# The order of SyncE's transfer queue in the convolution module of a two-layer diffusion trunk

## The chip, the cores and the metric

The kernel runs on one core of a Trainium2 chip. The metric is device time in microseconds (us) of one execution, as the median of several; three runs of the kernel before gave 1317.1, 1321.2 and 1324.15 us. The profile is of one further execution. Engines are named as in the profile: PE (TensorE, matrix products), DVE (VectorE), ACT (ScalarE), POOL (GpSimd) and SP (SyncE, whose queue issues the transfers).

## The reference

Two layers over 256 tokens of width 1024, in float32. Layer 0 is a mixer (mLSTM heads and differential attention) and a dense SwiGLU. Layer 1 is a Conformer convolution module and a top-2-of-8 expert SwiGLU. The change is in the convolution module, of which this is the core:

```
u = modulate(x, mix_pre_g, sh_m, sc_m)
a, g = jnp.split(u @ pw1_w + pw1_b, 2, axis=-1)
h = a * jax.nn.sigmoid(g)
h = depthwise_conv(h, dw_w) + dw_b          # 31 taps along the tokens, per channel
h = jax.nn.silu(layernorm(h, ln_g, ln_b))
y = h @ pw2_w + pw2_b
```

After it come the norm, the router, and the experts, whose weights (eight experts of three matrices) are most of what the kernel reads.

## The kernel before

**Weights.** All weights lie in HBM as units of 128 x 2048 floats (1 MB). `raw` (L330) asks for a unit with one transfer issued by SP, into a ring of six buffers ("raw" and "raw2" in the rows). `half` (L363) splits half a unit into a high part (ACT, L372, tile `whi`) and a low part (DVE, L373, tile `wlo`), and PE multiplies with both. `Ahead` (L380) keeps a list of such halves for the first projection pw1, eight units of two halves: `step` makes the next half, asking for its unit with the first, and `get` returns a half that is due. Five halves are made before the stage, so each step makes the half that PE uses five products later. A buffer is asked for anew once DVE has taken both halves out of it (or, for a unit of taps, PE).

**The stage (L1422 to L1481).** The channels are eight blocks k of 128. The loop over `jj` = 0 to 3 computes two blocks of `a` and two of `g` a turn, in four products of half a unit (24 matmuls each). After the first product of the next turn, `glu(jj - 1)` forms a * sigmoid(g) for blocks k = 2 jj - 2 and 2 jj - 1: ACT makes the sigmoid (L1416, L1417), DVE multiplies into `hp[k]` (L1418).

**The depthwise convolution.** Blocks 0 and 1 are convolved on DVE: `conv_v` (L1359) is one tensor_scalar (L1361) and 30 scalar_tensor_tensor (L1364), which are queued as "background" and put between other work by `fill(n)`, n at a time. Blocks 2 to 7 are convolved on PE: `conv_shift(k)` (L1343) writes `hp[k]` to a scratch tile `hd` in HBM (L1345) and reads it back four times, shifted by 0 to 3 tokens, into `x4` (L1348, "B<-hd" in the profile); `conv(k)` (L1350) then multiplies it with a unit of taps, 64 matmuls in the trace. `x4` has three buffers, k modulo 3. The units of taps `w4s[jj]` are asked for at the start of turns 1, 2 and 3.

**What follows a block.** `convolved` (L1381) takes the results. After the second of them, a product with `on` (in the trace "mm<-B,on") gives their mean over channels, the pilot, which ACT copies (L1399) and DVE subtracts from both (L1401); every later block has it subtracted as it leaves PSUM (L1390). The first two are blocks 0 (from DVE) and 2 (from PE). `sums` adds up each block and its square on PE ("aux<-B,one", "aux<-m,one").

**What sets the order.** A scheduler places the instructions of every engine by priorities and dependencies, except where `in_order` stands around them: there the named engines keep the order of the source. Around this stage it names PE, DVE and ACT. SP is not named, so the transfers stand where the scheduler put them. Each engine works its queue off strictly from the front, and SP's queue too: a transfer that waits for a semaphore holds up all that stand behind it. The units of the second projection pw2 are asked for outside this stretch of the source, and the scheduler may move them, and their halves, into it.

PE's order in the stage: pw1 for turns 0 to 2; the first unit of turn 3; conv(2), the pilot's product and its sums; the last unit of pw1; conv(3), conv(4), conv(5); then conv(6) and conv(7) with the sums between.

Of the kernel before, what the change touches and what calls it, by code (L numbers as in the profile page):

```python
# [11 lines left out]
F32 = mybir.dt.float32  # L12
# [7 lines left out]
P = 128  # L20
D = 1024
KT = D // P
T = 256
# [8 lines left out]
HW = T + 32  # L32
# [6 lines left out]
NV = 2  # L39
# [197 lines left out]
def build(ctx: ExitStack, tc: tile.TileContext, d, unit, dbg=None):  # L237
    nc = tc.nc
# [5 lines left out]
    def nm(s):  # L244
        ctr[0] += 1
        return f"{s}_{ctr[0]}"
# [83 lines left out]
    def raw(key, src=None, two=False):  # L330

        src = d["w"][unit[key]] if src is None else src
        tag = room.pop(0) if room else "raw"
        if tag in ("gp", "w", "xn", "pT"):
            if tag == "w":
                t = [ring("whi", F32, HW_), ring("wlo", F32, HW_)]
            else:
                t = [tl([P, HW_], "gp"), tl([P, HW_], "m4")] if tag == "gp" else [tl([P, HW_], tag, bufs=2) for _ in range(2)]
            for q in range(2):
                nc.sync.dma_start(t[q], src[:, HW_ * q : HW_ * q + HW_])  # L340
            return t
        t = ring("raw") if tag == "raw" else tl([P, UW], tag)
        if two:
            for q in range(2):
                nc.sync.dma_start(t[:, HW_ * q : HW_ * q + HW_], src[:, HW_ * q : HW_ * q + HW_])
        else:
            nc.sync.dma_start(t, src)
        return t[:, :HW_], t[:, HW_:]
# [148 lines left out]
    def fill(n=1000):  # L497

        while background and n > 0:
            if next(background[0], 0) == 0:  # L500
                background.pop(0)
            else:
                n -= 1
# [134 lines left out]
    ET = mybir.EngineType  # L638

    def in_order(*engines):  # L640
        return tc.manual_schedule(engines=set(engines or (ET.PE, ET.DVE, ET.Activation)))
# [119 lines left out]
    def wstat(half, out, n0, n1):  # L761
        h, l = by_k(half, KT)
        for k in range(KT):
            mm(out, h[:, k], uh[k][:, n0:n1], k == 0, False)
            mm(out, h[:, k], ul[k][:, n0:n1], False, False)
            mm(out, l[:, k], uh[k][:, n0:n1], False, k == KT - 1)
# [573 lines left out]
    cvo = tl([P, KT, T], "B8")  # L1340


    def conv_shift(k):  # L1343
        hd = hdram.tile([P, HW], F32, tag="hd", name=nm("hd"), bufs=4)
        nc.sync.dma_start(hd, hp[k])  # L1345
        x4 = x4s[k % 3]
        for j in range(4):
            nc.sync.dma_start(x4[32 * j : 32 * j + 32], hd[:, j : j + HW - 4].rearrange("(c p) t -> p c t", c=4))  # L1348

    def conv(k):  # L1350
        w4 = w4s[k // 2][k % 2].rearrange("p (b c) -> p b c", c=32)
# [53 lines left out]
    w4s = {}  # L1405
# [13 lines left out]
            if k < NV:  # L1419
                background.append(conv_v(k))  # L1420

    order = in_order()  # L1422
    order.__enter__()
    pp = None
    for jj in range(4):
        if jj >= NV // 2:
            w4s[jj] = raw(("taps", jj))
        prev, pp = pp, []
        for n in (jj, 4 + jj):
            p_ = pm("mm")  # L1430
            for j in range(2):
                ahead.step()
                wstat(ahead.get(("pw1", n), j), p_[:, T * j : T * j + T], 0, T)
                if prev:
                    glu(jj - 1, prev)
                    if jj > 1:
                        conv_shift(2 * jj - 2)
                    if jj != 3 and jj > 1:
                        conv_shift(2 * jj - 1)
                    prev = None  # L1440
                    fill(2)
                else:
                    fill(4)
            pp.append(p_)
            fence.close()
            if jj == 3 and n == jj:
                conv(2)
                drain(2)
                conv_shift(5)
    conv(3)  # L1450
    drain(2)
    glu(3, pp)
# [865 lines left out]
```

## Time and profile before

| | |
|---|---|
| median of three runs | 1321.2 us (1317.1 to 1324.15) |
| profiled execution | 1319.89 us, its span 1317.9 us |
| mean granted clock of PE in it | 0.978 of full speed |
| busy in the span | PE 1254.1 us (95%), DVE 633.0 (48%), ACT 431.2 (33%) |
| bytes | 406.41 MB, mean 308 GB/s |
| convolution stage | about 472 to 560 us of the span |

How to read it: PE is the engine that is nearly always busy, so a change counts for what it adds to or takes from PE's waits, or from the time in which PE runs at the lower clock. Times in a row are microseconds from the start of the span. "[4.00 <-DMA B<-hd]" behind a row is the time that the engine stood idle before it, and what ended it. "SPq" rows are issues of transfers: their length is what the issue takes and not the transfer, whose time to landing is listed apart. [...]

### The profile page before, as it was taken

What the parts mean: (1) busy time and instruction counts of PE and PEld (TensorE: products, weight loads), DVE (VectorE), ACT (ScalarE), POOL (GpSimd) and SP (SyncE); (2) the same over time, 40 slices, a digit from 0 to 9 for tenths busy, and PEclk for the clock granted to TensorE, in tenths of its full rate; (3) what the DMA queues carried; (4) which work ended last, traced back from release to release, by engine and by line L of the source; (5) the groups of instructions that cost most, each with busy time, mean ns of one, the idle gap of its engine ahead of it and who ended that gap; (6) DMA issues with size and microseconds to landing.
All of it is one profiled execution on the core that took longest, in us unless ns stands there. A gap on an engine that the chain in (4) does not pass through costs nothing. (4 is left out here: it accounts for less than half of the span.)

```text
span 1317.9 us, 22697 instructions
## 1 busy us (share of the span) xinstructions
PE 1254.1 (95%) x9256; PEld 807.2 (61%) x9256; DVE 633.0 (48%) x1049; ACT 431.2 (33%) x784; POOL 32.4 (2%) x83
## 2 busy tenths in 40 slices
PE   6999999999999998998999789999999999999996
PEld 5878777789998987674345333444434444678533
DVE  4689758698886668663102012011111121689422
ACT  4553346564444553262020000210001102567311
POOL 1000001100000010011000000000000000000000
PEclk9999999999999999997999899999999999999998
DMA  9727820478987627687769999999999996999994
GB/s 353 283 95 297 309 98 9 160 313 347 361 324 308 255 76 206 213 275 292 264 260 417 420 420 418 419 419 368 360 418 420 419 372 263 426 347 368 350 419 191
DMA packets 71089, 406.41 MB, mean 308 GB/s; under 512 B 7874, under 2 KB 12226, under 8 KB 31812
## 3 DMA queue, kind: packets, MB, share of 16 engines
q1 hardware_dynamic: 70980, 404.91, 78.5%
q8 instruction: 74, 1.21, 0.4%
q14 instruction: 35, 0.29, 0.1%
HBM read 402.94 MB, written 1.93 MB: 307 GB/s over the span
## 5 line engine op out<-in xcount | busy, mean ns | idle before, releaser
L373 DVE TENSOR_TENSOR wlo<-raw,whi 128x1024 fp32r<-128x1024 f32 x154 | 186.0, 1222 | 47.6 <-ACT whi L372 46.5
L282 PE MATMUL mm<-raw,gL 128*32 128x256 f32 (+3 forms) x1392 | 194.0, 438 | 4.5 <-DMA raw<-w 4.5
L372 ACT CAST whi<-raw 128x1024 fp32r<-128x1024 f32 x154 | 159.4, 1048 | 102.6 <-PE mm L282 64.3
L282 PE MATMUL mm<-B,whi 128*128 128x256 f32 x960 | 171.8, 282 | 0.2 <-DVE B L632 0.2
L282 PEld LDWEIGHTS mm<-B,whi 128*128 128x128 f32 x960 | 148.4, 189 | 2.3 <-PE mm L282 0.6
L282 PE MATMUL mm<-B,wlo 128*128 128x256 f32 x480 | 134.9, 281 | 0.0
L282 PE MATMUL mm<-B,gL 128*32 128x256 f32 (+3 forms) x808 | 124.4, 449 | 3.3 <-DMA B<-w 3.3
L282 PEld LDWEIGHTS mm<-raw,gL 128*32 128x32 f32 (+1 forms) x1392 | 77.9, 122 | 80.8 <-issue 57.5
L1887 DVE TENSOR_TENSOR cv<-cv,mm 64x512 f32<-64x512 f32 (+1 forms) x36 | 23.3, 647 | 191.4 <-ACT cv L1886 191.1
L1886 ACT ACTIVATE cv<-mm 64x512 f32<-64x512 f32 (+1 forms) x36 | 19.9, 553 | 280.9 <-PE mm L282 280.8
L282 PE MATMUL aux<-whi,pT 128*128 128x512 f32 (+2 forms) x400 | 100.9, 425 | 0.6 <-DMA whi<-w 0.6
L282 PEld LDWEIGHTS mm<-B,wlo 128*128 128x128 f32 x480 | 90.6, 189 | 0.0
L282 PEld LDWEIGHTS mm<-B,gL 128*32 128x32 f32 (+1 forms) x808 | 46.7, 123 | 55.3 <-issue 40.8
L282 PE MATMUL aux<-raw,pT 128*32 128x256 f32 (+1 forms) x592 | 77.6, 470 | 1.6 <-DMA raw<-w 0.9
L282 PE MATMUL aux<-wlo,pT 128*32 128x256 f32 (+2 forms) x284 | 69.1, 429 | 1.9 <-DVE wlo L373 1.1
L1903 DVE COPY pT<-aux 128x384 f32<-128x384 f32 (+4 forms) x42 | 19.0, 453 | 107.8 <-PE aux L1896 99.1
L282 PEld LDWEIGHTS aux<-whi,pT 128*128 128x128 f32 (+2 forms) x400 | 49.5, 158 | 25.5 <-issue 13.2
L282 PE MATMUL mm<-U,whi 128*128 128x256 f32 (+1 forms) x240 | 64.5, 331 | 0.0
L282 PE MATMUL aux<-B,pT 128*32 128x256 f32 (+2 forms) x424 | 59.7, 467 | 0.0
L282 PE MATMUL mm<-whi,B 128*128 128x512 f32 (+1 forms) x192 | 58.4, 380 | 0.0
L282 PE MATMUL mm<-whi,gL 128*32 128x256 f32 (+3 forms) x336 | 55.9, 452 | 2.3 <-DMA whi<-w 2.3
L282 PE MATMUL mm<-wlo,gL 128*32 128x256 f32 (+3 forms) x336 | 53.9, 445 | 0.2 <-DMA wlo<-w 0.2
(467 smaller groups left out, 1866.9 us busy)
## 6 DMA issues: line engine op xcount, KB each, us to landing
raw<-w SPq DMA_DIRECT2D x237, 1024.0 KB, 7.5
B<-w SPq DMA_DIRECT2D x69, 1024.0 KB, 11.2
whi<-w SPq DMA_DIRECT2D x52, 512.0 KB, 11.3
wlo<-w SPq DMA_DIRECT2D x52, 512.0 KB, 10.9
gp<-w SPq DMA_DIRECT2D x18, 512.0 KB, 10.1
m<-w SPq DMA_DIRECT2D x18, 512.0 KB, 10.0
B<-hd SPq DMA_DIRECT2D x24, 142.0 KB, 5.3
x<-x SPq DMA_DIRECT2D x2, 512.0 KB, 4.4
```

The source lines that it names most:

```text
L282: PE.matmul(out, lhsT, rhs, start=start, stop=stop)
L372: A.copy(hi, rq)
L373: V.tensor_tensor(lo, rq, f(hi), ALU.subtract)
L1886: A.activation(s, p_[:64, :w], AF.Silu)
L1887: V.tensor_tensor(s, s, p_[64:, :w], ALU.mult)
L1903: V.tensor_copy(h[:, :o], pt[:, :o])
```

## The change

`in_order` now names SP too, so that the transfers of the stage stand in the order of the source. The source is rearranged: `conv_shift` takes several blocks, and issues all their writes before their reads; in the product after which `glu` stands, the half that is due is fetched first, then come `glu` and `conv_shift`, and only then the next step ahead; the units of taps are asked for at the end of turns 1, 2 and 3 instead of their start. What is computed, and the order on PE, is the same.

```diff
-    def conv_shift(k):
-        hd = hdram.tile([P, HW], F32, tag="hd", name=nm("hd"), bufs=4)
-        nc.sync.dma_start(hd, hp[k])
-        x4 = x4s[k % 3]
-        for j in range(4):
-            nc.sync.dma_start(x4[32 * j : 32 * j + 32], hd[:, j : j + HW - 4].rearrange("(c p) t -> p c t", c=4))
+    def conv_shift(*ks):
+        hds = []
+        for k in ks:
+            hd = hdram.tile([P, HW], F32, tag="hd", name=nm("hd"), bufs=4)
+            nc.sync.dma_start(hd, hp[k])
+            hds.append(hd)
+        for k, hd in zip(ks, hds):
+            x4 = x4s[k % 3]
+            for j in range(4):
+                nc.sync.dma_start(x4[32 * j : 32 * j + 32], hd[:, j : j + HW - 4].rearrange("(c p) t -> p c t", c=4))
...
-    order = in_order()
+    order = in_order(ET.PE, ET.DVE, ET.Activation, ET.SP)
     order.__enter__()
     pp = None
     for jj in range(4):
-        if jj >= NV // 2:
-            w4s[jj] = raw(("taps", jj))
         prev, pp = pp, []
         for n in (jj, 4 + jj):
             p_ = pm("mm")
             for j in range(2):
-                ahead.step()
-                wstat(ahead.get(("pw1", n), j), p_[:, T * j : T * j + T], 0, T)
                 if prev:
+                    W_ = ahead.get(("pw1", n), j)
                     glu(jj - 1, prev)
                     if jj > 1:
-                        conv_shift(2 * jj - 2)
-                    if jj != 3 and jj > 1:
-                        conv_shift(2 * jj - 1)
+                        conv_shift(*range(2 * jj - 2, 2 * jj - (jj == 3)))
+                    ahead.step()
+                    wstat(W_, p_[:, T * j : T * j + T], 0, T)
                     prev = None
                     fill(2)
                 else:
+                    ahead.step()
+                    wstat(ahead.get(("pw1", n), j), p_[:, T * j : T * j + T], 0, T)
                     fill(4)
...
+        if jj >= NV // 2:
+            w4s[jj] = raw(("taps", jj))
     conv(3)
```

SP's queue in the middle of the stage. Before: `raw2_917` and `raw_931` are units of taps, `raw_925` is the last unit of pw1, `raw_973` and `raw2_986` are units of pw2, `hd` is the scratch and `B8 <- hd` a shifted read into `x4`.

```order
L347 DMA raw2_917_4847<-w 128x2048
L347 DMA raw_925_4900<-w 128x2048
L347 DMA raw_931_4995<-w 128x2048
L347 DMA raw_973_5514<-w 128x2048
L347 DMA raw2_986_5583<-w 128x2048
L1345 DMA hd_923_4886<-B8_882_4572 128x288
L1345 DMA hd_924_4892<-B8_882_4572 128x288
L1348 DMA B8_886_4578<-hd_923_4886 32x4x284 x4
L1348 DMA B8_884_4576<-hd_924_4892 32x4x284 x4
```

After: `raw2_916` and `raw_930` are taps, `raw2_924` is the last unit of pw1, `raw2_986` a unit of pw2.

```order
L347 DMA raw2_916_4845<-w 128x2048
L1347 DMA hd_920_4856<-B8_882_4572 128x288
L1347 DMA hd_921_4858<-B8_882_4572 128x288
L1352 DMA B8_886_4578<-hd_920_4856 32x4x284 x4
L1352 DMA B8_884_4576<-hd_921_4858 32x4x284 x4
L347 DMA raw2_924_4898<-w 128x2048
L347 DMA raw_930_4993<-w 128x2048
L347 DMA raw2_986_5583<-w 128x2048
L1347 DMA hd_934_5004<-B8_882_4572 128x288
```

The last unit of pw1 stood five places ahead of the first scratch write and now stands behind both writes and all eight reads; no unit of pw2 stands ahead of these writes any more.

DVE's queue, a little before that: `wlo` are low halves of pw1, L1364 (before) and L1368 (after) taps of conv_v, and L1418 (before) and L1422 (after) the multiplications of glu(1), which fill `hp[2]` and `hp[3]`. Before:

```order
L373 TENSOR_TENSOR wlo_916_4816<-raw2_914_4813,whi_915_4815 128x1024
L1364 SCALAR_TENSOR_TENSOR B8_887_4579<-B8_882_4572,col_5_68,B8_887_4579 128x256 x4
L373 TENSOR_TENSOR wlo_920_4851<-raw2_914_4813,whi_919_4850 128x1024
L1418 SCALAR_TENSOR_TENSOR B8_882_4572<-mm_903_4707,col_5_68,cv_921_4878 128x256
L1418 SCALAR_TENSOR_TENSOR B8_882_4572<-mm_903_4707,col_5_68,cv_922_4882 128x256
```

After:

```order
L373 TENSOR_TENSOR wlo_915_4814<-raw_913_4811,whi_914_4813 128x1024
L1368 SCALAR_TENSOR_TENSOR B8_887_4579<-B8_882_4572,col_5_68,B8_887_4579 128x256 x4
L1422 SCALAR_TENSOR_TENSOR B8_882_4572<-mm_902_4705,col_5_68,cv_918_4848 128x256
L1422 SCALAR_TENSOR_TENSOR B8_882_4572<-mm_902_4705,col_5_68,cv_919_4852 128x256
L373 TENSOR_TENSOR wlo_923_4869<-raw_913_4811,whi_922_4868 128x1024
```

glu(1) now stands ahead of the half that it stood behind.

DVE's queue further on, up to the end of conv_v(0): the tensor_scalar in the last row is the first of conv_v(1). Here `wlo_927` and `wlo_930` (before), `wlo_926` and `wlo_929` (after) are the two halves of the last unit of pw1, and `wlo_975` and `wlo_977` halves of a unit of pw2. Before:

```order
L373 TENSOR_TENSOR wlo_927_4903<-raw_925_4900,whi_926_4902 128x1024
L1364 SCALAR_TENSOR_TENSOR B8_887_4579<-B8_882_4572,col_5_68,B8_887_4579 128x256 x4
L373 TENSOR_TENSOR wlo_930_4936<-raw_925_4900,whi_929_4935 128x1024
L1364 SCALAR_TENSOR_TENSOR B8_887_4579<-B8_882_4572,col_5_68,B8_887_4579 128x256 x3
L373 TENSOR_TENSOR wlo_975_5517<-raw_973_5514,whi_974_5516 128x1024
L1364 SCALAR_TENSOR_TENSOR B8_887_4579<-B8_882_4572,col_5_68,B8_887_4579 128x256 x4
L373 TENSOR_TENSOR wlo_977_5521<-raw_973_5514,whi_976_5520 128x1024
L1364 SCALAR_TENSOR_TENSOR B8_887_4579<-B8_882_4572,col_5_68,B8_887_4579 128x256
L1418 SCALAR_TENSOR_TENSOR B8_882_4572<-mm_918_4849,col_5_68,cv_933_5022 128x256
L1418 SCALAR_TENSOR_TENSOR B8_882_4572<-mm_918_4849,col_5_68,cv_934_5026 128x256
L1364 SCALAR_TENSOR_TENSOR B8_887_4579<-B8_882_4572,col_5_68,B8_887_4579 128x256 x3
L1361 TENSOR_SCALAR B8_887_4579<-B8_882_4572,col_5_68 128x256
```

After:

```order
L373 TENSOR_TENSOR wlo_926_4901<-raw2_924_4898,whi_925_4900 128x1024
L1368 SCALAR_TENSOR_TENSOR B8_887_4579<-B8_882_4572,col_5_68,B8_887_4579 128x256 x4
L373 TENSOR_TENSOR wlo_929_4934<-raw2_924_4898,whi_928_4933 128x1024
L1368 SCALAR_TENSOR_TENSOR B8_887_4579<-B8_882_4572,col_5_68,B8_887_4579 128x256 x8
L1422 SCALAR_TENSOR_TENSOR B8_882_4572<-mm_917_4847,col_5_68,cv_932_4996 128x256
L1422 SCALAR_TENSOR_TENSOR B8_882_4572<-mm_917_4847,col_5_68,cv_933_5000 128x256
L1368 SCALAR_TENSOR_TENSOR B8_887_4579<-B8_882_4572,col_5_68,B8_887_4579 128x256 x3
L1365 TENSOR_SCALAR B8_887_4579<-B8_882_4572,col_5_68 128x256
```

The two halves of pw2 are gone from here (they and two more now stand much later, between the results of conv(5) and conv(6)), and 15 taps of conv_v(0) still stand behind the first half of pw1's last unit.

## Rows read from the trace of the kernel before

**Rows 1.** Page, part 5: one group, its count | busy, mean ns | idle before, releaser
```profile
L372 ACT CAST whi<-raw 128x1024 fp32r<-128x1024 f32 x154 | 159.4, 1048 | 102.6 <-PE mm L282 64.3
```

**Rows 2.** Timeline of PE, 511 to 549: start, us, operation [idle before <-releaser]
```profile
511.98 0.28 PE L282 MATMUL mm<-B,wlo 128*128 128x256 f32 x1
...
516.26 5.24 PE L282 MATMUL mm<-B,raw 128*32 128x256 f32 x64 [4.00 <-DMA B<-hd]
...
521.43 1.36 PE L282 MATMUL mm<-B,on 128*128 128x256 f32 x4
...
523.71 0.62 PE L282 MATMUL aux<-B,one 128*32 128x256 f32 x2 [0.92 <-DVE B L1401]
...
525.04 0.50 PE L282 MATMUL mm<-B,whi 128*128 128x256 f32 x2
...
530.91 10.57 PE L282 MATMUL mm<-B,raw 128*32 128x256 f32 x192
...
545.11 3.66 PE L282 MATMUL mm<-B,raw 128*32 128x256 f32 x64 [1.57 <-DMA B<-hd]
```

**Rows 3.** Timeline of SP's queue, 480 to 543: start and time of issues
```profile
480.44 23.84 SPq L347 DMA_DIRECT2D raw<-w  x5
...
504.39 0.84 SPq L1345 DMA_DIRECT2D hd<-B  x2
...
511.43 3.65 SPq L1348 DMA_DIRECT2D B<-hd  x8
...
535.54 1.27 SPq L1345 DMA_DIRECT2D hd<-B  x2
...
537.82 4.94 SPq L1348 DMA_DIRECT2D B<-hd  x8
```

**Rows 4.** Transfers issued at 504.4, 512.4, 535.5, 497.8, 543.1: KB each, us to landing
```profile
hd<-B SPq DMA_DIRECT2D x1, 144.0 KB, 7.0
...
B<-hd SPq DMA_DIRECT2D x1, 142.0 KB, 3.2
...
hd<-B SPq DMA_DIRECT2D x1, 144.0 KB, 2.2
...
raw<-w SPq DMA_DIRECT2D x1, 1024.0 KB, 4.7
...
raw<-w SPq DMA_DIRECT2D x1, 1024.0 KB, 7.0
```

**Rows 5.** Timeline of DVE, 502 to 553: start, us, line, operation, count
```profile
502.71 1.22 DVE L373 TENSOR_TENSOR wlo<-raw,whi 128x1024 fp32r<-128x1024 f32 x1
...
503.84 0.87 DVE L1418 SCALAR_TENSOR_TENSOR B<-mm,col,cv 128x256 f32<-128x256 f32 x2
...
506.67 2.04 DVE L1364 SCALAR_TENSOR_TENSOR B<-B,col,B 128x256 f32<-128x256 f32 x4
...
511.21 1.22 DVE L373 TENSOR_TENSOR wlo<-raw,whi 128x1024 fp32r<-128x1024 f32 x1
...
518.05 0.41 DVE L1361 TENSOR_SCALAR B<-B,col 128x256 f32<-128x256 f32 x1
...
523.90 4.13 DVE L1364 SCALAR_TENSOR_TENSOR B<-B,col,B 128x256 f32<-128x256 f32 x8
...
552.71 0.48 DVE L1390 SCALAR_TENSOR_TENSOR B<-mm,col,m 128x256 f32<-128x256 f32 x1 [2.61 <-PE aux L282]
```

**Rows 6.** Windows of 1 us: busy by engine, then granted clock, DMA share, GB/s
```profile
517.00:518.00 1.00, 1.00 (x16) 0.51 (x12) 0.93 (x3) 0.00 (x0) 0.00 (x0) 0.50 1.04 251
...
520.00:521.00 1.00, 1.00 (x24) 0.67 (x20) 0.00 (x0) 0.00 (x0) 0.00 (x0) 1.00 0.93 352
```

**Rows 7.** The same in windows of 2 us, later
```profile
598.00:600.00 2.00, 2.00 (x11) 2.00 (x11) 0.00 (x0) 0.75 (x2) 0.00 (x0) 0.50 1.02 430
```

**Rows 8.** Waits of SP's queue, 600 to 700: us in total, times, longest
```profile
SPq L347 <- PE mm L282: 53.2, 6, 19.2
```

**Rows 9.** One window of 40 us: busy by engine, clock, DMA share, GB/s
```profile
730.00:770.00 40.00, 27.34 (x293) 12.48 (x287) 1.95 (x6) 1.02 (x3) 0.00 (x0) 0.79 1.02 420
```

## The prediction

> **What bounds the kernel now.** I read the table of the page first (PE is busy for 95% of the span), then the timelines of PE, SP's queue and DVE over the convolution stage, then the transfers one by one, and last the granted clock in narrow windows. On PE the reader is to see one large hole: its last product before conv(2) ends at 511.98 + 0.28 = 512.26, conv(2) starts at 516.26 after 4.00 us of waiting for "DMA B<-hd", the shifted reads, and takes 5.24 us for 64 matmuls, where three convolutions later take 10.57 us, or 3.52 each [rows 2]. [...] So the late reads cost 4.00 + 1.72 = 5.7 us. SP's queue shows why they are late: the two scratch writes are issued at 504.39, the reads only from 511.43 [rows 3], since a write took 7.0 us to land where another, at 535.5, took 2.2 [rows 4]. The order shows a unit of pw2 (1 MB) issued just ahead of the slow ones.
>
> DVE is not the bound, but it has no slack here: halves, taps and GLU stand back to back from 502.71 to 518.05, where conv_v(0) has ended and the first operation of conv_v(1) starts [rows 5]. The pilot's product, which needs conv_v(0) as well as conv(2), starts at 521.43, 3.4 us later [rows 2]. That 3.4 us is all the room that DVE has before PE waits for it.
>
> **The change part by part.** Its own time is that of the profiled execution, 1319.9 us, which lies 1.3 us below the median of the three runs, 1321.2; I add the sum to the median.
>
> *GLU ahead of a half.* glu(1) no longer stands behind a low half on DVE. A low half takes 503.84 - 502.71 = 1.13 us of the queue [rows 5], so the first write goes out at 504.39 - 1.13 = 503.3 [rows 3].
>
> *Writes and reads ahead of the units.* With no 1 MB unit in front the write lands after 2.2 us and not 7.0 [rows 4]: at 505.5. Eight reads are issued in 3.65 us [rows 3], so the first four, which conv(2) needs, are out by 507.3, and land about 3.2 us later [rows 4], at 510.5. PE comes there at 512.26: the wait and the slow clock go, conv(2) ends at 512.26 + 3.52 = 515.8 in place of 521.5. A gain of 5.7 us, if nothing else is late.
>
> *The last unit of pw1.* Something is. This unit was the second of the five issues that begin at 480.44 [rows 3]; now it stands behind both writes and all eight reads, so it cannot be issued before 505.5 + 3.65 = 509.2. Its landing has two bounds: 4.7 us with the queue to itself (the unit at 497.8), and 7.0 for the unit at 543.1 that was issued behind eight reads [rows 4], which themselves stood behind another unit. I take 6.2, nearer to the second, because it has the same eight reads in front and only the other unit is missing. It lands at 515.4, within 513.9 to 516.2.
>
> [...]
>
> *Who waits for it.* ACT's cast of its first half takes 1.05 us [rows 1], and DVE's low half follows. DVE's queue is strict: in the order, 15 taps of conv_v(0) and glu(2) stand behind that low half. DVE comes there at about 505.6 (the low half and two taps behind glu(1)) and stands idle for ten microseconds. From the landing to the end of conv_v(0) it needs: cast 1.05; low half 1.13; four taps 1.96 (506.67 to 508.63 is such a row and the next); low half 1.13; eight taps 4.1; glu(2) 0.8; three taps 1.4 [rows 5]. That is 11.6 us, so conv_v(0) ends at 515.4 + 11.6 = 527.0 where it ended at 518.05.
>
> *PE.* conv(2) is done at 515.8, and PE's next instruction is the pilot's product. It starts at 527.0 and not at 521.43: 5.6 us later than before, after a hole of 11 us. All products of the last unit of pw1 stand behind it on PE, and conv(3) to conv(5) behind these. GLU(2)'s scratch writes, which leave at about 525, have until conv(4) at 542 and hide.
>
> *The clock.* Before, the hole of 4.00 us was followed by about 3.3 us at 0.50 [rows 2, 6]. The pilot's product (1.36 us) and its sums (1.3 us) now fall into such a stretch and may take twice as long [rows 2]: at least nothing, at most, by that row, 2.7. I take 2.0. Then the products of the last unit start 7.6 us late, at 532.6 in place of 525.04.
>
> [...]
>
> *The halves of pw2.* Four low halves of pw2 now stand between the results of conv(5) and conv(6) on DVE; before, the first was at 511.21 and all four stood among work that no one waited for [rows 5]. After glu(3) and its 12 and 8 taps they cost 4 x 1.13 = 4.5 us at the point where PE needs conv(6)'s and conv(7)'s results. I follow DVE from conv(3), which ends at 532.6 + 5.9 + 3.5 = 542.0: GLU(3) until 543.4, 12 taps 549.5, a result and 8 taps 554.0, two small ones 554.8, four halves 559.3, the bias of pw2 560.5, the result of conv(6) and small ones 561.8. Then comes conv(7)'s result, which stood at 552.71 [rows 5]: 9.1 us later, 1.5 more than the 7.6. The reads for conv(7) now stand behind a 1 MB unit of their own and come out at about the same place. I take 9.3 for the stage.
>
> *Behind the stage.* Nothing gives it back: between 600 and 700 SP's queue waits 53.2 us for PE to free buffers [rows 8], so the experts' transfers move with PE, and what is late here stays late.
>
> Sum: - 5.7 (hole and clock at conv(2)) + 11.3 (the new hole, 515.8 to 527.0, of which 5.6 remain against the old start) + 2.0 (clock) + 1.7 (end of the stage) = + 9.3. On 1321.2 that is 1330.5 us; I say 1330.
>
> **Rivals.**
>
> *Faster: the reads in time, and the unit in time.* If the last unit of pw1 reaches DVE before it is missed, only the 5.7 us are left: 1315.5 us. For it speaks the hole on PE, the only large one in the stage. Against it: for no loss at all the unit would have to land by 509.8 (521.43 - 11.6), and for the whole gain by 504.2 (515.8 - 11.6), while SP cannot issue it before the first write, at 503.3, and not before that write has landed and the reads are out. The point that decides is the unit's landing time.
>
> *Absorbed.* Later, between 730 and 770, PE is busy for only 27.34 of 40 us while the DMA share is 1.02 [rows 9]: there it waits for the experts' weights. If these transfers kept their old times, the 9.3 us would vanish in that wait, and the time would be 1321 to 1324. Against it speak the 53.2 us by which SP's queue waits for PE just before [rows 8]. It would take a queue that runs ahead of PE by more than its buffers.
>
> *The clock stays low.* If after 11 us of idleness the clock stays at 0.50 through the products of the last unit (5.9 us at full speed), as it did later beside a busy PE [rows 7], another 4 to 6 us come on top: 1335 to 1337. The two holes ahead of conv(6) and conv(7) could do the same once more.
>
> **How the numbers follow.** The forecast (all of the 9.3 us, within its own bounds) has 0.62. Its own range: with the landing at 513.9, no loss to the clock, and the 1.57 us wait ahead of conv(6) [rows 2] recovered, it is 1321.2 + 4.1 - 1.6 = 1323.7; with the landing at 516.2, 2.7 for the clock and 2.5 at the end it is 1333. Absorbed, wholly or in part: 0.18. The clock stays low: 0.13. Faster: 0.07. A change of 0.5%, 6.6 us, is about what a measurement of this kernel can tell from none. Above 1327.8 lie about 0.57 of the forecast and the 0.13 of the low clock: slower 0.70. Within it lie the rest of the forecast, nearly all of the absorbed case, and part of the faster one: same 0.24. Faster by more than 0.5%: 0.06. For 8 in 10 the range goes from 1320 to 1337: it leaves out the faster case, a little of the absorbed one and the far end of the low clock.
>
> **What would show it.** Right: a landing of the last pw1 unit near 515 and, on ACT and DVE, a wait of some 10 us for it; conv(2) starting at 512 without a wait and taking 3.5 us; PE waiting for DVE (L1368 or the pilot's chain) for about 11 us afterwards, and 0.50 in the clock behind it; the low halves of pw2 after 550 on DVE. Wrong: a hole still ahead of conv(2); the unit landing by 510, or the pilot's product at 522 or sooner; or an unchanged start of the experts' stage in spite of a late pilot.

## The result, and the profile after

The changed kernel takes 1338.93 us (median of four runs, 1335.74 to 1340.58) where the kernel before takes 1322.68 (four runs): a ratio of 1.0118, 95% interval 1.0098 to 1.0137. That is slower by 16.25 us; 9.3 were forecast, and the range ended at 1337. The profiled execution took 1340.58 us, its span 1338.4, and is the longest of the four; that of before took 1319.89, 2.8 us under its median.

PE's timeline of the changed kernel, to be read against [rows 2]: start, us, operation, and in brackets the idle time ahead of it with what ended it.

```profile
515.23 3.66 PE L282 MATMUL mm<-B,raw 128*32 128x256 f32 x64
...
532.32 2.04 PE L282 MATMUL mm<-B,on 128*128 128x256 f32 x4 [13.43 <-DVE B L1368]
...
537.06 0.80 PE L282 MATMUL mm<-B,whi 128*128 128x256 f32 x2
...
544.48 10.57 PE L282 MATMUL mm<-B,raw 128*32 128x256 f32 x192
...
558.42 3.66 PE L282 MATMUL mm<-B,raw 128*32 128x256 f32 x64 [1.30 <-DMA B<-hd]
...
566.83 5.35 PE L282 MATMUL mm<-B,raw 128*32 128x256 f32 x64 [4.33 <-DMA B<-hd]
...
581.15 0.63 PE L282 MATMUL aux<-whi,B 128*128 128x512 f32 x1
```

The hole ahead of conv(2) is gone, and conv(2) runs at full clock (the granted clock, a share of full speed, is 1.00 from 515 to 519). In its place stand 13.43 us ahead of the pilot's product (line 2), then 4.33 us ahead of conv(7) with a slow conv(7) behind it (5.35 us; the granted clock is 0.50 from 568 to 571). The last row is the first product of pw2, at the lower clock (0.63 us where the trace of before shows 0.50): the granted clock is 0.50 again from 578 to 585.

All times here are 3 us later than in the trace of before already when conv(2) becomes due, and this has arisen ahead of the stage: its first product starts at 471.99 before and at 475.03 after. The cause of this shift is not known. So I measure from one point, the end of the last product ahead of conv(2): 512.26 before, 515.30 after. The row of this product in the changed kernel:

```profile
515.02 0.28 PE L282 MATMUL mm<-B,wlo 128*128 128x256 f32 x1
```

And, from the kernel before, the rows of conv(7)'s last product and of pw2's first:

```profile
552.27 0.38 PE L282 MATMUL mm<-B,raw 128*32 128x256 f32 x1
...
560.51 0.50 PE L282 MATMUL aux<-whi,B 128*128 128x512 f32 x1
```

Counted from that point:

| us from that point | pilot's product | last pw1 unit | conv(7) ends | pw2 starts |
|---|---|---|---|---|
| before | 9.2 | 12.8 | 40.4 | 48.3 |
| after | 17.0 | 21.8 | 56.9 | 65.9 |
| later by | 7.9 | 9.0 | 16.5 | 17.6 |
| forecast | 5.6 | 7.6 | | 9.3 |

From pw2 on the distance between the two traces stays about the same to the end (20.6 us of shift at pw2, 20.4 at the last product). The whole loss of the change lies in the stage: half of it up to the last pw1 unit (9.0), half behind it (8.6).

SP's queue in the changed kernel, as in [rows 3] (start and time of the issues):

```profile
506.26 0.80 SPq L1347 DMA_DIRECT2D hd<-B  x2
508.05 4.95 SPq L1352 DMA_DIRECT2D B<-hd  x8
513.10 13.16 SPq L347 DMA_DIRECT2D raw<-w  x3
...
549.12 0.34 SPq L1347 DMA_DIRECT2D hd<-B  x1
549.50 0.84 SPq L347 DMA_DIRECT2D raw<-w  x1
...
553.77 0.35 SPq L1347 DMA_DIRECT2D hd<-B  x1
555.49 0.35 SPq L347 DMA_DIRECT2D raw<-w  x1
558.59 2.71 SPq L1352 DMA_DIRECT2D B<-hd  x4
```

Transfers issued at 506.3, 513.1, 553.8, 555.5 and 558.6 (the last number is the time to landing), against [rows 4]:

```profile
hd<-B SPq DMA_DIRECT2D x1, 144.0 KB, 1.7
...
raw<-w SPq DMA_DIRECT2D x1, 1024.0 KB, 7.3
...
hd<-B SPq DMA_DIRECT2D x1, 144.0 KB, 4.8
...
raw<-w SPq DMA_DIRECT2D x1, 1024.0 KB, 8.6
...
B<-hd SPq DMA_DIRECT2D x4, 142.0 KB, 6.6
```

The first write lands in 1.7 us; the last pw1 unit, behind eight reads, needs 7.3. At the end of the stage the write for conv(7) stands behind one pw2 unit (549.50; the four reads for conv(6) lie between) and its reads behind a second (555.49): 4.8 us to land, and 6.6 instead of 3.2.

DVE in the changed kernel, against [rows 5]:

```profile
521.59 1.23 DVE L373 TENSOR_TENSOR wlo<-raw,whi 128x1024 fp32r<-128x1024 f32 x1 [12.97 <-ACT whi L372]
...
529.87 0.87 DVE L1422 SCALAR_TENSOR_TENSOR B<-mm,col,cv 128x256 f32<-128x256 f32 x2
...
560.81 4.62 DVE L373 TENSOR_TENSOR wlo<-raw,whi 128x1024 fp32r<-128x1024 f32 x4
...
566.70 0.48 DVE L1394 SCALAR_TENSOR_TENSOR B<-mm,col,m 128x256 f32<-128x256 f32 x1
...
572.25 0.48 DVE L1394 SCALAR_TENSOR_TENSOR B<-mm,col,m 128x256 f32<-128x256 f32 x1 [4.29 <-PE mm L282]
```

DVE stands idle for 13 us ahead of the late unit's low half. At the end it is not DVE that is late: conv(7)'s result (last row) waits for PE, which waits for the reads.

### The profile page after: what moved, and what is told of

The parts are those of the page before. It is cut to its first block, busy times and chain, and to the rows that moved or that the text cites. A ratio compares the mean times of both kernels' runs of the same rounds, so it can differ in the third digit from the quotient of the medians.

```text
span 1338.4 us, 22685 instructions
## 1 busy us (share of the span) xinstructions
PE 1263.4 (94%) x9256; PEld 811.6 (61%) x9256; DVE 633.1 (47%) x1049; ACT 430.5 (32%) x784; POOL 32.4 (2%) x83
```

## The experiments

Each is compared with the kernel before on its own chip. The column "stage" is from each trace: the start of pw2 from the same point as above, less the 48.3 us of before.

| run | median, us | before, us | ratio (95%) | stage |
|---|---|---|---|---|
| e1_unit_first | 1331.7 | 1323.1 | 1.0061 (1.0036 to 1.0086) | +8.9 |
| e2_order_alone | 1348.1 | 1323.1 | 1.0196 (1.0162 to 1.0229) | +24.2 |
| e3_source_alone | 1320.5 | 1323.1 | 0.9974 (0.9957 to 0.9991) | -2.8 |
| e4_pw2_behind | 1340.3 | 1323.1 | 1.0115 (1.0075 to 1.0155) | +17.8 |
| e6_places | 1326.7 | 1323.5 | 1.0028 (1.0011 to 1.0044) | +2.6 |
| e7_warm | 1336.9 | 1323.5 | 1.0110 (1.0081 to 1.0139) | +9.1 |
| e8_reads_split | 1334.1 | 1323.5 | 1.0085 (1.0056 to 1.0113) | +10.3 |
| e9_taps_first | 1328.6 | 1323.5 | 1.0044 (1.0025 to 1.0064) | +9.2 |
| e10_all_places | 1323.2 | 1323.6 | 0.9997 (0.9986 to 1.0008) | +0.5 |
| e11_halves_after | 1339.7 | 1323.6 | 1.0122 (1.0107 to 1.0137) | +16.5 |
| e12_units_last | 1319.7 | 1323.2 | 0.9978 (0.9964 to 0.9992) | -2.5 |
| e13_pw2_early | 1335.6 | 1323.2 | 1.0102 (1.0077 to 1.0127) | +14.1 |
| e14_half_first | 1332.8 | 1322.3 | 1.0069 (1.0053 to 1.0086) | +11.2 |
| e15_best | 1319.9 | 1322.3 | 0.9973 (0.9960 to 0.9985) | -4.2 |

The stage accounts for the time of nearly every run within 2 us. The exceptions are e7 and e9, whose profiled executions took 1332.8 and 1333.6 us, 4 us under and 5 us over their medians.

**Which half of the change costs.** Theory A: two transfers at wrong places. Rivals: B, an ordered queue costs by itself; C, the rearranged source costs.

```diff
 e2: only the order, on the kernel before
-    order = in_order()
+    order = in_order(ET.PE, ET.DVE, ET.Activation, ET.SP)
 e3: only the source, on the kernel after
-    order = in_order(ET.PE, ET.DVE, ET.Activation, ET.SP)
+    order = in_order()
```

Expected of e2: 

> The kernel before with SP named in the in-order stretch, and no line of the source moved. Theory A: the last unit of pw1 again stands behind the writes and reads of blocks 2 and 3, which are now write, reads, write, reads, so it lands later still: PE waits 13 us or more ahead of the pilot's product, + 14 to + 25 us on the kernel before. Rival C (the rearranged source costs: GLU ahead of a half, the taps later): within 3 us of the kernel before.

Expected of e3: 

> The changed source, with SP left to the scheduler. Its queue has the last unit of pw1 and a unit of pw2 ahead of the scratch writes again. Theory A: no wait for DVE ahead of the pilot's product, the 4 us hole ahead of conv(2) is back; within 3 us of the kernel before. Rival C: + 8 us or more.

PE ahead of the pilot's product in e2:

```profile
540.42 2.04 PE L282 MATMUL mm<-B,on 128*128 128x256 f32 x4 [18.01 <-DVE B L1364]
```

PE at conv(2) in e3:

```profile
516.82 3.66 PE L282 MATMUL mm<-B,raw 128*32 128x256 f32 x64 [1.89 <-DMA B<-hd]
```

With the source as it was, the order alone costs more than the whole change; the new source under the old scheduler is a little faster than before, with half of the hole ahead of conv(2) left. C falls: the rearranged source softens what the order costs.

**The pilot.** Four runs on the changed kernel: the unit asked for ahead of the writes (e1), four reads ahead of it in place of eight (e8), DVE's taps ahead of its low half (e9), and 32 products of 512 columns that nothing uses in the hole (e7).

```diff
 e1:          w4s[jj] = raw(("taps", jj))
+        if jj == 1:
+            ahead.got[("pw1", 7)] = raw(("pw1", 7))   # Ahead.step takes it from here
 e8: (step, then conv_shift(3) at the next half)
-                        conv_shift(*range(2 * jj - 2, 2 * jj - (jj == 3)))
+                        conv_shift(2 * jj - 2)
 e9:
-                    fill(2)
+                    fill(18 if jj == 2 else 2)
-                    fill(4)
+                    fill(0 if jj == 2 else 4)
 e7:
+            warm(32)
             pmu = pm("mm")
```

Expected of e1: 

> The changed kernel, with the last unit of pw1 asked for at the end of turn 1, ahead of the scratch writes of blocks 2 and 3; nothing else moves. Theory A (two misplaced transfers: this unit behind the reads, and the reads for conv(7) behind a unit of pw2): the wait of PE for DVE ahead of the pilot's product falls from 13.4 us to under 2, since conv_v(0) ends about 516.8 + the lateness that the run brings to the stage; the clock stays at 1.00 there; the hole ahead of conv(7) stays. Time within + 0 to + 4 us of the kernel before, 12 to 16 us under the changed one. Rival B (keeping SP's queue in order costs by itself, in every transfer of the stage): most of the loss stays, more than + 10 us on the kernel before.

Expected of e8: 

> The changed kernel with the write and reads for conv(3) asked for behind the last pw1 unit: only one write and four reads stand ahead of the unit instead of two and eight. Theory A: the unit is issued about 2.6 us earlier (near 510.5 in place of 513.1) and lands in 6 to 7 us, the pilot's product starts 3 to 4 us earlier (near 528.5), and the time falls by 3 to 5 us to 1334 to 1336; conv(7)'s hole stays. Rival (the landing time does not depend on the reads ahead, the pilot waits for something else on VectorE): pilot within 1 us of 532, time 1338 to 1340.

Expected of e9: 

> The changed kernel with SyncE's queue as it is; only VectorE's order differs: the 15 taps of conv_v(0) that stood behind the low half of the late pw1 unit, and behind glu(2), are taken ahead of that low half, into the 10 us in which VectorE stood idle. The unit still lands at about 520.4. Theory A (it is VectorE's strict queue that turns the late unit into the late pilot): conv_v(0) ends at about 515, the pilot's product follows conv(2) at 519 in place of 532, TensorE then waits only some 1 to 2 us for the unit's first half (near 523), and the clock does not fall to 0.5 for long; a wait of 0 to 5 us ahead of conv(4) may appear, because a pw2 unit stands ahead of its write, and conv(7)'s hole stays. 7 to 12 us less than the changed kernel: 1327 to 1332. Rival G (the late unit costs its lateness whatever VectorE does): the products of the last unit start no earlier than 530 and the time is 1336 to 1340.

Expected of e7: 

> The changed kernel with 32 products of 512 columns into a spare bank between conv(2) and the pilot's product, in the 13 us hole; nothing uses them. Nothing else moves. If the low clock behind the hole is a price of the hole's idleness (Theory A prices it at 2.7 us: the pilot's product takes 2.04 us instead of 1.36, its sums and the first products twice as long), the granted clock stays near 1.00 through 545 and the time falls by 2 to 3.5 us, to 1335.5 to 1337. Rival: the clock falls there for another reason (the transfers or the power of the whole chip), the granted clock at 530 to 540 stays at 0.5 and the time within 1 us of the changed kernel, 1338 to 1340. It becomes slower only if the 32 products outlast the hole (they need 11 to 12 us at full clock).

In e1 the pilot's product starts 4.0 us after conv(2) is due: its wait is gone. The time did not fall as far as expected, though. The waits of PE in e1, 505 to 580 (total, times, longest), and SP's issues there:

```profile
PE mm L282 <- DMA B<-hd: 12.2, 3, 4.8
```

```profile
531.25 0.35 SPq L347 DMA_DIRECT2D raw<-w  x1
531.66 2.50 SPq L1352 DMA_DIRECT2D B<-hd  x4
```

The scheduler, free to place what stands outside the ordered stretch, had put a pw2 unit between the write for conv(5) and its reads; the unit waited for a buffer until 531.25, and the reads with it.

In e8 the unit went out at 511.60, landed in 6.9 us, and the pilot came 14.5 us after the point in place of 17.0. The pilot's part was as expected in direction and smaller (2.5 us, 3 to 4 expected); the rest of the 4.8 us came from a shorter wait at conv(7) (1.9). In e9 SP's queue is that of the changed kernel, and the pilot starts 8.6 us earlier:

```profile
522.90 2.08 PE L282 MATMUL mm<-B,on 128*128 128x256 f32 x4 [4.85 <-ACT cv L1420]
```

The unit is as late as ever (ACT's cast of it starts 5.2 us behind the point in both), so what made it expensive is DVE's strict queue; the time lies in the range expected. What is left, 4.85 us, is ACT's: glu(2) stands there behind the casts of the late unit. Rival G (the lateness costs itself) falls.

In e7 the pilot and its sums ran at full clock:

```profile
530.40 1.02 PE L282 MATMUL mm<-B,on 128*128 128x256 f32 x4
```

From the pilot to the last unit's first product it is 3.3 us (before 3.6, after 4.7). The clock does fall here too, to 0.50 from 521.6 to 525, right behind the 3.9 us for which PE still stood idle ahead of the 32 products (the first nine of them take 3.91 us, the 24 that the trace has between 525 and 530 take 5.96); it rises while they run, and is 0.99 to 1.00 from 525 to 540. So the low clock that the changed kernel has at the pilot came with the long hole: with these products in it the clock there is 1.00, without them 0.50. The 32 products took 9.2 us in all, less than the 11 to 12 expected at full clock (the 23 products of this form in the trace of before keep PE busy for 8.5 us, 0.37 each, which is 11.8 for 32). By the time this is inconclusive: the median lies 2.0 us under the changed kernel's, as expected, but the runs spread over 6.4 us, and the profiled one waited 1.7 us at conv(7) where the changed kernel waited 4.3, which is not the clock's doing.

**The end of the stage.** Five runs. e4 asks for all pw2 units behind the reads for conv(7); e11 also puts the halves of two behind conv(7)'s result; e13 asks for these two at 538, behind the taps of turn 3, and for the rest behind the reads; e14 exchanges the first of them with the taps.

```diff
 e4:     conv_shift(7)
+    for j in range(2):
+        for c in range(2):
+            po.got[c, j] = raw(("pw2", c, j))       # po.split takes it from here
 e11: e4, and behind conv(7) and drain():
+    po.split(0, 0)
+    po.split(0, 1)
 e13: ahead of conv(3) (split(0, 1) ahead of conv(6), the rest behind conv_shift(7)):
+    for j in range(2):
+        po.got[0, j] = raw(("pw2", 0, j))
+    po.split(0, 0)
 e14: e13, with the first unit ahead of the taps:
+            if jj == 3:
+                po.got[0, 0] = raw(("pw2", 0, 0))
             w4s[jj] = raw(("taps", jj))
```

Expected of e4: 

> The changed kernel, with the four units of pw2 asked for behind the reads of block 7. Theory A: the 4.3 us wait of PE ahead of conv(7) and the low clock behind it go, conv(7) follows conv(6) within 2 us; 4 to 7 us under the changed kernel, + 9 to + 12 on the kernel before, unless PE then waits for pw2's halves. Rival D (the reads of block 7 are late because of GLU(3) and the scratch write alone): the wait ahead of conv(7) stays above 3 us and the time is that of the changed kernel, + 16, or above.

Expected of e11: 

> The changed kernel with the four pw2 units asked for behind the reads for conv(7), as in the earlier run, and now the halves of the first two of them also put behind conv(7)'s result on VectorE. In the earlier run conv(7) came 5.4 us sooner than in the changed kernel, yet pw2's first product started at 581.4 against 581.2: VectorE split two halves ahead of conv(7)'s result, TensorE waited 3.4 us for that, and its clock fell to 0.50. Theory A (that wait and the clock behind it took back what the reads had won): without them pw2 starts near 576 and the time falls 4 to 6 us below the changed kernel, to 1333 to 1335. Rival H (what follows conv(7) is bound by something else, the statistics or pw2's late units): pw2 starts at 580 to 582 again, and the time stays at 1338 to 1340.

Expected of e13: 

> The changed kernel up to conv(5), late pilot included; only the end of the stage differs. The first two pw2 units that need halves are asked for right behind the taps of turn 3 (near 540, where SyncE stood idle for 9 us and their buffers are free), their halves made ahead of conv(3)'s and of conv(6)'s result on VectorE; the other two pw2 units and the first expert units stand behind the reads for conv(7). So neither the reads nor the halves are late. Theory A (the end of the stage cost 7 us in the changed kernel, by the reads and, where these were mended, by the halves): conv(6) and conv(7) start without a wait over 1 us, no wait for halves or the copy of the sums follows, pw2 starts near 575 in place of 581, and the time is 1331 to 1334. Rival H (what follows conv(7) is bound by something else): pw2 starts at 580 or later and the time is 1337 to 1340.

Expected of e14: 

> As the run with two pw2 units asked for early, with one exchange: the first of them stands ahead of the taps of turn 3 and not behind them, so that it lands by 542 or so and its halves are made while VectorE is idle (540 to 548), not ahead of a result that is ready. In that run the unit landed near 546, conv(3)'s result and all behind it came 2.2 us late, and TensorE waited 3.9 us for conv(5)'s result. Theory A (the end of the stage cost its 7 us by places in the queues alone): no wait over 1 us from the pilot to pw2, 3 to 4 us less than that run's 1335.6: 1331 to 1333, which is where the forecast stood without the end of the stage. Rival H (the stage's end is bound by something else, and mending one wait brings up the next): another wait of 2 us or more, time 1334.5 or more.

PE at the end of the stage in e4:

```profile
561.42 3.69 PE L282 MATMUL mm<-B,raw 128*32 128x256 f32 x64
...
568.98 1.06 PE L282 MATMUL aux<-B,one 128*32 128x256 f32 x2 [3.44 <-DVE B L1394]
...
581.38 0.63 PE L282 MATMUL aux<-whi,B 128*128 128x512 f32 x1
```

SP's queue there (the write for conv(7) and its reads):

```profile
553.39 0.35 SPq L1347 DMA_DIRECT2D hd<-B  x1
555.57 1.75 SPq L1352 DMA_DIRECT2D B<-hd  x4
```

With no unit ahead, and the four reads for conv(6) ahead as in the changed kernel, the write lands in 2.1 us in place of 4.8 and the reads in 2.9 in place of 6.6. conv(7) starts without a wait and ends 7.1 us earlier than in the changed kernel: it was the units that made its reads late, and rival D falls. But pw2 starts no earlier, and the time is that of the changed kernel: two halves of a pw2 unit that landed late stand on DVE ahead of conv(7)'s result, and the sums, and what follows them to pw2, run at the low clock (1.06 us for a pair of sums where it is 0.62 in the trace of before; the granted clock is 0.50 from 570 to 585). The expectation missed this. In e11 the halves were out of DVE's way and in ACT's; the wait is as long (PE, 505 to 600):

```profile
PE mm L282 <- ACT cvt L1500: 3.5, 1, 3.5
```

The copy of the sums stood behind casts that waited for the units. That was my placing; this expectation missed too. So did that of e13, where the halves were due too early:

```profile
548.08 2.36 DVE L373 TENSOR_TENSOR wlo<-raw,whi 128x1024 fp32r<-128x1024 f32 x2 [9.54 <-ACT whi L372]
```

The halves stood ahead of conv(3)'s result and held it back by some 3 us (to 550.36), and all of DVE's work behind it; PE waited 3.9 us for conv(5)'s result. With the unit a place further forward (e14) these halves start at 544.27, conv(6) and conv(7) start without a wait, and one wait of 1.88 us remains ahead of the sums of conv(5), where none over 1 us was expected. PE at these sums and at conv(7) in e14:

```profile
554.38 0.62 PE L282 MATMUL aux<-B,one 128*32 128x256 f32 x2 [1.88 <-DVE B L1394]
...
559.90 3.66 PE L282 MATMUL mm<-B,raw 128*32 128x256 f32 x64
```

The time, 1332.8, is as expected. From the last pw1 unit to pw2 it takes 37.2 us: 35.5 before, 44.1 after. So places in the queues, SP's and DVE's, made 6.9 of the 8.6 us that the end of the stage cost. Rival H, whose times e4 and e11 had shown, falls.

**Versions with every unit at a place of its own.** All four (e6, e10, e12, e15) keep e1's unit, and in e10 to e15 (but for e11) the first expert units too are asked for behind the reads for conv(7). e6 asks for two pw2 units at 511, e10 at 529.7, and both for the other two behind the reads for conv(7); e12 and e15 ask for all four there. From e10 on the taps of turn 3 stand beside those of turn 2, and the writes for conv(6) and conv(7) go out together (`conv_write` issues writes alone, `conv_shift` then only the reads). The halves of the first pw2 unit stand ahead of conv(3)'s result in e6, of conv(6)'s in e10 and of conv(7)'s in e12 and e15. The main lines of the edits:

```diff
 e6:      if jj == 2:
+            for c in range(2):
+                po.got[c, 0] = raw(("pw2", c, 0))
 e10:                 conv_shift(5)
+                for c in range(2):
+                    po.got[c, 0] = raw(("pw2", c, 0))
-    conv_shift(6)
+    conv_write(6, 7)
+    conv_shift(6)
 e12: e10 without the two units behind conv_shift(5), and with
     conv_shift(7)
+    for j in range(2):
+        for c in range(2):
+            po.got[c, j] = raw(("pw2", c, j))
     A.copy(srow, psum_[:, :T])
+    po.split(0, 1)
 e15: e12 with c as the outer loop there, and
     drain()
+    po.split(0, 1)
     A.copy(srow, psum_[:, :T])
```

Expected of e6: 

> SyncE stays in order, but every unit gets a place of its own: the last pw1 unit ahead of the first scratch writes (as in the run with the unit first), the first two pw2 units behind the taps of turn 2, where their buffers are already free and 5 us pass until the next write, the last two behind the reads for conv(7), and the halves of the first pw2 unit on VectorE ahead of conv(3)'s result, where it stood idle for 6.6 us. Theory A (two misplaced transfers): no wait of TensorE over 1 us on the shifted reads or on conv_v between 510 and 565; conv(2) starts 4 us earlier than before, the holes of 1.6 us ahead of conv(6) and of 5 us ahead of conv(7) are gone, the stage ends 3 to 6 us earlier than before: 1316 to 1320 us where before has 1323. Rival B (an ordered SyncE queue costs wherever it meets a wait): a new wait appears elsewhere and the time stays at 1328 or more. Rival F (what is won in the stage is lost behind it, because the last two pw2 units come late): stage shorter, but waits for weights at 565 to 590, and the time within 2 us of before.

Expected of e10: 

> SyncE in order, and no 1 MB unit within the 4 us ahead of a scratch write or between a write and its reads: the last pw1 unit stands ahead of the first writes; the taps of turn 3 with those of turn 2; the first two pw2 units behind the reads for conv(5); the writes for blocks 6 and 7 together, then their reads, and only behind these the last two pw2 units and the first three expert units; the halves of pw2 on VectorE ahead of conv(6) and of conv(7), where it stood idle. Theory A: each write lands in about 2 us, TensorE waits no more than 1 us for shifted reads at any of conv(2) to conv(7), the stage ends 5 to 8 us earlier than before, 1315 to 1319 us where before has 1323. Rival F (given back behind the stage): the stage is that much shorter, but pw2's products or the first experts wait for their units, and the time lies within 2 us of before. Rival B (an ordered SyncE queue costs somewhere whatever stands in it): a wait of more than 3 us in the stage, 1326 or more.

Expected of e12: 

> The run with all places mended except one: there the writes for blocks 6 and 7 were issued 2.6 us behind two pw2 units (529.7) and took 7.2 us to land, and conv(6) waited 4.3 us. Here all four pw2 units stand behind the reads for conv(7), the halves of the first on VectorE ahead of conv(7)'s result and those of the second behind the copy of the sums. Theory A: the writes for blocks 6 and 7 land within 2.5 us, conv(6) and conv(7) start without a wait over 1 us, conv(7) ends near 547 (554 in that run). What follows depends on the halves: if these units (landing near 541 to 550) come in time, pw2 starts near 557 to 558 where it started at 563.2, and the time is 1316 to 1319 where before has 1323.5. Rival F (the late pw2 units take it back, as in the two runs that put them behind the reads in the changed kernel): conv(7) ends at 547, but a wait of 2 to 5 us for halves follows, pw2 starts at 561 to 563 and the time is 1321 to 1324.

Expected of e15: 

> As the run with the units last, with one exchange: the second pw2 unit for which halves are made ahead of the statistics is asked for second and not third, and its halves stand directly behind conv(7)'s result, ahead of the copy of the sums. In that run the two low halves stood ahead of the statistics (553.3 in place of 551.9), TensorE waited 1.5 us for them, the granted clock fell to 0.50 from 553 to 563, and pw2 started at 559.4 with conv(7) ended at 547.5: 11.9 us, against 9.3 us where the clock stayed up. Theory A: no wait over 1 us after conv(7), clock 1.00 to 563, pw2 starts near 557, and with its first products at full speed 3 to 4.5 us are won: 1315 to 1317, where before has 1323. Rival (the clock falls there anyway, by the DMA share of 1.0 beside it): clock 0.50 from 553 again, 1319 to 1320.

e6 and e10 missed their ranges in the same way. SP's queue in e10:

```profile
529.68 0.86 SPq L347 DMA_DIRECT2D raw<-w  x2
532.26 0.81 SPq L1348 DMA_DIRECT2D hd<-B  x2
539.85 1.74 SPq L1355 DMA_DIRECT2D B<-hd  x4
```

Two units issued 2.6 us earlier held the writes for 7.5 us, and conv(6) waited 4.27; in e6 the write for conv(4), issued 3 us behind three units, took 8.5. SP's queue in e12, where no unit stands ahead:

```profile
531.47 0.86 SPq L1348 DMA_DIRECT2D hd<-B  x2
533.30 1.74 SPq L1355 DMA_DIRECT2D B<-hd  x4
```

These writes land in 1.8 us, and conv(7) ends 33.9 us after the point, 6.5 earlier than before. Then pw2's halves, ahead of the statistics, make PE wait 1.5 us, the clock is at 0.50 from 553 to 563, and 4.0 of the 6.5 us are gone by pw2: the time lies between the ranges of theory A and of rival F. e15 moved these halves; in its trace pw2 starts 1.7 us sooner, yet its median is that of e12, not the 1315 to 1317 expected but the time of its rival: a wait of 0.87 stayed, and the clock still fell to 0.50, from 558 to 561.

e12, e15 and e3 lie 0.2 to 0.3% under the kernel before, and so under the changed one, and cannot be told apart. In e12 and e15 SP's queue is as ordered as in the changed kernel, so order does not cost by itself (B falls).

## Why the prediction was wrong

The direction was forecast, and so was the mechanism of the first half of the loss. By the trace the stage lost 17.6 us and not 9.3: the pilot 7.9 (forecast 5.6), from there to the last unit's first product 1.1 (2.0), the end of the stage 8.6 (1.7).

- *Conv(2)*: right. It starts when due and takes 3.66 us, at a granted clock of 1.00 where before had 0.50 behind its hole [rows 6]; the forecast gain of 5.7 is 5.6 in the trace (4.00 of waiting, and 5.24 against 3.66 [rows 2]).
- *The last pw1 unit*: right in kind, short in size. Less the 3 us by which this trace runs late, it was issued at 510.1 (509.2 forecast), since the eight reads took 4.95 us to issue and not 3.65, and took 7.3 us to land, not 6.2 and above my upper bound of 7.0. The pilot: 7.9 later, not 5.6. The chain of 11.6 us on DVE held to a tenth (520.51, where ACT's cast starts, to 532.09). Nearer than my 6.2 was the upper bound, from the unit of the kernel before that went out behind eight reads. A unit landed in 7.3 us behind eight reads and in 6.9 behind four (e8), where the queue to itself gave 4.7 [rows 4].
- *The clock*: 2.0 us were forecast between the pilot's start and the last unit's first product, and it cost 1.1 there. It went on: the unit's own products took 1.6 us longer than before, since the clock was 0.50 until 540.6, nearly half of their time. So the rival of a clock that stays low came true in part, for 1.6 of its 4 to 6 us. PE ran at 0.50 for 8 us behind the hole of 13.4 us (532.3 to 540.6), and for 3.3 behind that of 4.0 [rows 2, 6]; in those 8 us it worked through the pilot, its sums and short waits. Whether these are why the clock stayed low so long was not tried.
- *The step that failed*, "The reads for conv(7) now stand behind a 1 MB unit of their own and come out at about the same place", and with it the 1.7 us for the end of the stage. I read the place of the reads in the queue and did not price the unit ahead of them, though I had just priced the same thing elsewhere [rows 4]. The end of the stage cost 8.6 us: 6.2 between the start of conv(6) and the end of conv(7) (the wait of 4.33 and, behind it, conv(7) at the low clock), 1.6 of low clock on the last unit's products (the item above), and 1.1 between conv(7) and pw2, where the clock fell again at 578; 0.3 were won back ahead of conv(6). That the units ahead of the write and of the reads made the wait is shown by e4, which takes them away. DVE's four low halves, on which I spent the paragraph, cost nothing in this kernel: conv(7)'s result waited for PE. They are second in line: e4 and e11 mended the reads and met them. With both mended (e14) the end costs 1.8 us, most of it the clock on the last unit's products, and the time is 10.5 us over the kernel before, near the forecast.
- *Nothing given back*: right. One window of the changed kernel, as in [rows 9], and below it SP's waits from 600 to 700, as in [rows 8]:

```profile
730.00:770.00 40.00, 33.39 (x422) 16.19 (x418) 7.38 (x15) 3.03 (x7) 0.00 (x0) 0.91 1.02 419
```

```profile
SPq L347 <- PE mm L282: 41.9, 5, 19.6
```

PE has more work in the window than before, but only because the stretch with the waits comes later. Moved by 20.5 us, to 750.5 to 790.5, the window shows PE busy for 27.26 us, where before has 27.34 [rows 9], and SP's waits from 620 to 720 come to 53.1 us, where before has 53.2 [rows 8]. The transfers still wait for PE.

## What to carry to other kernels

A strict queue makes everything behind a late transfer late, whether or not it needs that transfer (13.4 us at the pilot in the changed kernel, 4.85 in e9): so for each moved transfer list what stands behind its first user on every engine, and for each short transfer on the critical path, how many megabytes were issued ahead of it and how recently (144 KB landed in 1.8 us in e12, and in 7.5 in e10, 2.6 us behind two units of 1 MB). Fixing the order of a queue for part of a program fixes only what is named there; look where the scheduler then puts the rest. And mend waits in pairs: the wait behind the one you see may be as long (4.33 us ahead of conv(7) in the changed kernel; with that gone, 3.44 ahead of the sums in e4).

## What was not expected of the hardware

- A 144 KB write to HBM landed in 1.7 to 2.2 us when nothing had been issued in the 7 us ahead of it (1.7 in the changed kernel, 2.2 in the kernel before [rows 4]), and later behind units of 1 MB, in these runs the more so the fresher they were. Behind one: 3.1 us when it was issued 4.8 us earlier (e1), 4.8 at 4.3 us with four reads between (the changed kernel), 7.6 at 0.8 us with four reads ahead of it (e6). Behind two, 6.4 to 7.5 (e10); behind three, 8.5 (e6). Four reads alone, 2.5 us ahead, made 2.1 to 2.3 (e4, e11, e13, e14). The 4 us that e10's expectation allowed were too few.
- Products that need no operand of the late unit waited too: the pilot's product in e9 for 4.85 us, and those of e7 for 3.88, for what the traces name as ACT's operations of glu(2) (L1420, L1421). Why they wait for these was not tried.
- In e12 the granted clock began to fall while PE was busy without a gap, half a microsecond ahead of the 1.5 us wait, as these windows show (busy by engine, then granted clock, DMA share, GB/s):

```profile
551.00:552.00 1.00, 1.00 (x11) 0.96 (x9) 0.98 (x1) 0.94 (x1) 0.00 (x0) 1.00 1.00 410
552.00:553.00 1.00, 1.00 (x10) 1.00 (x10) 1.00 (x2) 0.00 (x0) 0.00 (x0) 0.93 0.99 418
553.00:554.00 1.00, 0.37 (x2) 0.27 (x2) 0.90 (x5) 0.00 (x0) 0.00 (x0) 0.50 1.01 426
```

PE was then at the router's products of 8 columns. In e10 it did the same work at 1.00, with as high a DMA share beside it (0.98 to 1.01). In the changed kernel the clock fell at 578 and in e15 at 558, both a little further on in the same work, with PE busy for 1.00 of every microsecond from 573 and from 554 on. What decides there stays open.
